# A fused encoder step on one NeuronCore: the first set of FF1 products in two parts, six of eight pairs of feature tiles first

## The chip, the cores and the metric

One Trainium2 chip, one of its cores. The metric is the device time of one execution in microseconds (us); every time below is of that kind. A change of 0.2% is 5.3 us.

## The reference, cut to what matters

One layer of a streaming encoder over 640 tokens (512 of a prompt, 8 x 16 of a decode step), model width 2048, feed-forward width 5632, all in float32:

```
o = concat(rmsnorm(oa, norm_grp_a), rmsnorm(ob, norm_grp_b))
x = x + o @ w_out
h = rmsnorm(x, norm_ffn)
x + (silu(h @ w_gate) * (h @ w_up)) @ w_down
```

`oa` and `ob` are the outputs of two groups of attention heads. What matters here is the seam between `o @ w_out` (the out-projection) and the first product with `w_gate`.

## The kernel before, in words

**Operands.** A float32 product is made of three matmuls (`mm3`, lines 175 to 179): each operand is split into a high part `hi` (ScalarE, line 168) and a rest `lo` (VectorE, line 169), and hi x hi (line 177), hi x lo (line 178) and lo x hi (line 179) are summed in one PSUM bank. Splitting weights gives two tiles of 128 x 1024, splitting activations two of 128 x 320.

**Out-projection.** The second half of the out-projection (lines 833 to 849) makes 16 feature tiles `m` in the order 0, 8, 1, 9, ..., 7, 15. Each takes 48 matmuls over eight operand tiles (`own_a`, 16 slots in SBUF), writes two banks of the PSUM pool `dn`, and is then read out by VectorE (line 841), added to the residual `x2[m]` (line 842), stored, and squared and summed (line 247 on ScalarE, line 248 on GpSimd). In time the last three tiles are m = 14, m = 7 and m = 15.

**Preparing pairs.** FF1 multiplies by Strassen's scheme in its seven-product form: the 16 feature tiles are taken as eight pairs (`kt`, `kt + 8`), each token row is cut in two halves, and every pair gives seven left operands (`prepare`, lines 798 to 831): two scalings by the gain on ScalarE (line 802), four additions on VectorE (lines 820, 821, 823, 825), and seven splits. A left operand fills one SBUF slot, so a pair needs seven. Pairs 0 to 4 are prepared inside the out-projection, as soon as both tiles of the pair are there. Pairs 5, 6 and 7 are prepared step by step between the first seven FF1 products (`prep`, line 911; pair 7 in place, in its own `x2` tiles and one more).

**The FF1 products.** `quartet` (lines 856 to 908) loads four weight blocks of 512 KB (`get`, line 876), forms combinations of them (lines 889 and 891 on VectorE, 893 and 900 on GpSimd) and yields seven products in the order p1, p6, p7, p2, p5, p4, p3. Each product splits its weights into two slots of a list `H` (four slots at first, six after the first set), then runs 8 x 3 = 24 matmuls, one triple for each pair, so the first set is 168 matmuls. p1 and p5 lie in one two-bank tile of `dn`, p6 and p3 in another, p7, p2 and p4 in single banks of the pool `at` (four banks). After each product its bank is read out (line 949 on ScalarE, line 910 on VectorE). The first set is `w_gate` of FF tile pair 0; behind it come the sums for the norm (line 221, matmuls of one column, and later line 233, which spreads the result), then the set `w_up` of the same pair, which begins with its own p1 and p6.

**Slots set the order of the loads.** SBUF slots come from first-in-first-out lists: `n.get` takes the oldest free slot, `n.put` appends one, in the order of the program text. `W` (128 x 1024) holds weight blocks and the copies that `prepare` works on; a load into a slot starts when the last reader of the slot's former tile is done. At the first set the list has eight slots; call them A and B (the raw buffers of the out-projection's weights) and a0 to a5. In program order the blocks b12, b22, b11 and the combination s6 take A, B, a4 and a5, pairs 5 and 6 take a0, a1 and a2, a3, and b21 takes A again once b12 is split. The set `w_up` then gets A and B for b12 and b22, a0 (pair 5's) for b11 and a2 (pair 6's) for b21.

**Queues.** All loads and stores are issued by SyncE's one queue, in order. The framework under the kernel orders each engine's instructions at build time: by program order as priority and by a modelled time of readiness. On the chip each engine's queue runs in that order.

Of the kernel before, what the change touches and what calls it, by code (L numbers as in the profile page):

```python
# [8 lines left out]
ALU = mybir.AluOpType  # L9
# [6 lines left out]
KT = 16  # L16
TOK = 640
HT = 320
# [251 lines left out]
def build(nc, tc, io, pools):  # L270
    n = Net(nc, tc, io, pools)
    dma = nc.sync.dma_start
# [522 lines left out]
    more = group_operands(oa_d, g_a, ssq_a, range(4, 8))  # L795
    own_a, acts_a = own_a + more[0], acts_a + more[1]

    def prepare(kts, in_place=()):

        work = []  # L800
        for kt in kts:
            scale = lambda t, m: nc.scalar.activation(t[:, :TOK], x2[m], AF.Identity, scale=g_ffn[:, m:m + 1])
            if kt in in_place:
                a, c, e = x2[kt], x2[kt + 8], n.get("S")
                s1, s2 = e[:, :HT], e[:, HT:]
                drop = ("S", a, c, e)
            else:
                a, c = n.get("W"), n.get("W")
                s1, s2 = a[:, TOK:TOK + HT], c[:, TOK:TOK + HT]
                drop = ("W", a, c)  # L810
            scale(a, kt)
            scale(c, kt + 8)
            if kt not in in_place:
                n.put("S", x2[kt], x2[kt + 8])
            work.append((a[:, :HT], a[:, HT:TOK], c[:, :HT], c[:, HT:TOK], s1, s2, hs[kt], drop))
        tt = nc.vector.tensor_tensor
        for which in (0, 1, 2, 4, 3, 5, 6):
            for a11, a21, a12, a22, s1, s2, out, _ in work:
                if which == 1:
                    tt(s1, a21, a22, ALU.add)  # L820
                    tt(s2, s1, a11, ALU.subtract)
                elif which == 2:
                    tt(a11, a21, a11, ALU.subtract)
                elif which == 6:
                    tt(a12, a12, s2, ALU.subtract)
                t = n.get("S")
                out[which] = t, pack(t, HT)
                n.split((a11, s2, a11, s1, a12, a22, a12)[which], *out[which][1])
            yield which
        for w in work:  # L830
            n.put(*w[-1])

    hs = [[None] * 7 for _ in range(8)]
    x2 = [None] * KT
    for i, m in enumerate(m for kt in range(8) for m in (kt, kt + 8)):
        ps = n.dense([(io["w_out_a"][m], 8)], acts_a)
        if i == 0:
            n.rstd(ssq_a, 1024, r_a)
        d, x2[m] = n.get("S"), n.get("S")
        dma(out=x2[m], in_=x2_d[m])  # L840
        nc.vector.tensor_tensor(halves(d), ps, halves(r_a), ALU.mult)
        nc.vector.tensor_tensor(x2[m], x2[m], d, ALU.add)
        n.put("S", d)
        n.add_square(ssq, x2[m], i == 0, "S")
        dma(out=x2_d[m], in_=x2[m])
        if m >= 8 and m - 8 < 5:
            for _ in prepare([m - 8]):
                pass
    n.put("S", r_a, ssq_a, *own_a)


    n.move("WH", "H", 4)
    n.move("WR", "W1", 2)
    n.lists["W"] = n.lists.pop("W1") + n.lists["W"]

    def quartet(k, load, lefts, before=None, after=None, part="all"):

# [1 line left out]
        def product(src, which, bank):  # L861
            own = n.get("H"), n.get("H")
            hl = [r(sh(x, k, P)) for x in own]
            n.split(sh(src, k, P), *hl)
            if before:
                before(which)
            for j in range(k):
                n.mm3(bank, (hl[0][:, j], hl[1][:, j]), lefts[j][which][1], j == 0, j == k - 1)
            n.put("H", *own)
            if after:  # L870
                after(which)
            return bank
# [8 lines left out]
        if part == "late":  # L881
# [2 lines left out]
                yield name, product(src, which, n.bank()[:, :HT])  # L884
                n.put("W", src)
            return
        x, y = n.banks(), n.banks()
        b12, b22, b11 = get(1), get(3), get(0)
        nc.vector.tensor_tensor(b12[:, w], b12[:, w], b22[:, w], sub)  # L889
        s6 = n.get("W")  # L890
        nc.vector.tensor_tensor(s6[:, w], b11[:, w], b12[:, w], sub)  # L891
        yield "p1", product(b11, 0, x[:, 0])
        nc.gpsimd.tensor_tensor(b11[:, w], b22[:, w], s6[:, w], sub)  # L893
        yield "p6", product(s6, 1, y[:, 0])
        yield "p7", product(b12, 2, n.bank()[:, :HT])
        n.put("W", b12)
        b21 = get(2)
        if part == "all":
            yield "p2", product(b21, 4, n.bank()[:, :HT])
        nc.gpsimd.tensor_tensor(b21[:, w], b21[:, w], s6[:, w], sub)  # L900
        n.put("W", s6)
        yield "p5", product(b11, 3, x[:, 1])
        n.put("W", b11)
        yield "p4", product(b21, 5, n.bank()[:, :HT])
        n.put("W", b21)
        if part == "all":
            yield "p3", product(b22, 6, y[:, 1])
        n.put("W", b22)

    add = lambda o, a, b: nc.vector.tensor_tensor(o, a, b, ALU.add)  # L910
    prep = prepare([5, 6, 7], [7])
    lefts = [[None] * 7 for _ in range(NPAIR)]

    def fetch(j, which, raw=None, engine=nc.gpsimd):
# [25 lines left out]
    for i in range(NPAIR):  # L940
        for src in ("w_gate", "w_up"):
# [2 lines left out]
            y = n.get("S"), n.get("S")  # L944
            c11, c21, c12, c22 = y[0][:, :HT], y[0][:, HT:], y[1][:, :HT], y[1][:, HT:]
            start, end = i == 0 and src == "w_gate", i == NPAIR - 1 and src == "w_up"
            for step, bank in quartet(8, load, hs, (lambda w: next(prep)) if start else None, free if end else None):
                if step == "p1":
                    nc.scalar.activation(c11, bank, AF.Identity)
                elif step == "p6":  # L950
# [241 lines left out]
```

## Time and profile before

| | us |
|---|---|
| median of 3 runs | 2664.4 (2662.84 to 2664.69) |
| the profiled execution | 2662.34 |
| its span in the trace | 2660.6 |

TensorE's mean granted clock in the profiled execution was 0.992 of full speed. In the rows, PE is TensorE's matmuls, DVE VectorE, ACT ScalarE, POOL GpSimd, SPq SyncE's queue of transfers. A row of a timeline has its start and its length in us; the bracket at its end gives the engine's idle time just before it and what ended it. S, W, dn and at in a row are the lists and pools named above (H slots are W tiles too).

### The profile page before, as it was taken

The numbers are of one execution on the slowest core, as the hardware profiler recorded it, in microseconds if no ns is written. First come the engines' busy times: TensorE is split into PE (matmuls) and PEld (weight loads), VectorE is DVE, ScalarE is ACT, GpSimd is POOL, SyncE is SP. The second block draws the span as 40 slices with busy tenths as digits, with TensorE's granted clock in tenths as the row PEclk, the third lists the DMA queues.
The fourth block names the chain that finished last, engine by engine and source line by source line (L and its number), as shares of the span: only waits on it lengthen the run. The fifth ranks groups of instructions, "written<-read, shape, count | busy, mean of one in ns | idle before, by whom it ended". The sixth has DMA issues, their size and how long they took to land.

```text
span 2660.6 us, 44831 instructions
## 1 busy us (share of the span) xinstructions
PE 2588.9 (97%) x17565; PEld 2532.0 (95%) x17565; DVE 1916.3 (72%) x2961; ACT 1086.3 (41%) x1767; POOL 765.2 (29%) x553
## 2 busy tenths in 40 slices
PE   8999999999999999999999999999999999999986
PEld 8999998999899989999999999999999999999986
DVE  5665566656866887667667666676678888888897
ACT  5443344434634543333333333333334444444443
POOL 0000000000211223433343343334335434344454
PEclk9999999999999999999999999999999999999998
DMA  5322232433655433333333333323335744444344
GB/s 173 104 75 79 89 99 93 130 117 132 218 181 186 154 114 105 114 105 107 113 105 107 126 104 106 122 97 113 114 100 173 223 134 129 133 133 126 109 114 141
DMA packets 154147, 332.23 MB, mean 125 GB/s; under 512 B 18064, under 2 KB 69264, under 8 KB 153936
## 3 DMA queue, kind: packets, MB, share of 16 engines
q1 hardware_dynamic: 153936, 329.38, 39.1%
q8 instruction: 138, 2.26, 0.4%
q14 instruction: 73, 0.60, 0.1%
HBM read 274.38 MB, written 54.20 MB: 123 GB/s over the span
## 4 chain that ended last, share of the span: by engine, by line
PE 72%; DVE 6%; DMA 3%; issue 2%; ACT 1%; DVEq 0%; POOL 0%; SPq 0%; ACTq 0%
PE dn L177 15%; PE dn L179 15%; PE dn L178 14%; PE at L177 9%; PE at L178 9%; PE at L179 9%; DVE W L169 2%; DMA S<-act_d 1%; PE at L289 1%; DVE S L910 1%; DMA W<-w_down 1%; DVE S L1081 1%; ACT W L168 0%; DVE S L923 0%; PE at L365 0%
## 5 line engine op out<-in xcount | busy, mean ns | idle before, releaser
L177 PE MATMUL dn<-S,W 128*128 128x320 f32 x3694 | 1161.5, 314 | 14.8 <-ACT S L922 5.7
L179 PE MATMUL dn<-S,W 128*128 128x320 f32 x3694 | 1148.3, 311 | 11.1 <-DVE W L169 10.9
L178 PE MATMUL dn<-S,W 128*128 128x320 f32 x3694 | 1146.8, 310 | 2.0 <-DVE S L169 1.1
L168 ACT ACTIVATE W<-W 128x1024 fp32r<-128x1024 f32 (+2 forms) x632 | 608.8, 964 | 1051.3 <-PE dn L178 532.1
L169 DVE TENSOR_TENSOR W<-W,W 128x1024 fp32r<-128x1024 f32 (+2 forms) x632 | 766.1, 1212 | 150.0 <-ACT W L168 145.8
L177 PEld LDWEIGHTS dn<-S,W 128*128 128x128 f32 x3694 | 697.4, 189 | 28.4 <-issue 8.5
L179 PEld LDWEIGHTS dn<-S,W 128*128 128x128 f32 x3694 | 697.1, 189 | 15.9 <-DVE W L169 14.7
L178 PEld LDWEIGHTS dn<-S,W 128*128 128x128 f32 x3694 | 697.3, 189 | 4.7 <-DVE S L169 1.3
L179 PE MATMUL at<-S,W 128*128 128x320 f32 x1594 | 493.6, 310 | 6.7 <-DVE W L169 6.5
L177 PE MATMUL at<-S,W 128*128 128x320 f32 x1594 | 493.0, 309 | 0.0
L178 PE MATMUL at<-S,W 128*128 128x320 f32 x1594 | 492.7, 309 | 0.0
L893 POOL TENSOR_TENSOR W<-W,W 128x1024 f32<-128x1024 f32 (+2 forms) x76 | 163.4, 2149 | 583.1 <-DVE W L169 481.4
L179 PEld LDWEIGHTS at<-S,W 128*128 128x128 f32 x1594 | 299.3, 188 | 8.9 <-DVE W L169 8.7
L177 PEld LDWEIGHTS at<-S,W 128*128 128x128 f32 x1594 | 299.6, 188 | 0.3 <-ACT W L168 0.3
L178 PEld LDWEIGHTS at<-S,W 128*128 128x128 f32 x1594 | 299.4, 188 | 0.0
L910 DVE TENSOR_TENSOR S<-S,dn 128x320 f32<-128x320 f32 x358 | 164.0, 481 | 97.8 <-PE dn L179 96.5
L889 DVE TENSOR_TENSOR W<-W,W 128x1024 f32<-128x1024 f32 (+2 forms) x76 | 134.1, 1764 | 97.1 <-DMA W<-w_up 51.1
L900 POOL TENSOR_TENSOR W<-W,W 128x1024 f32<-128x1024 f32 (+2 forms) x76 | 166.4, 2190 | 111.0 <-DVE W L169 105.9
L910 DVE TENSOR_TENSOR S<-S,at 128x320 f32<-128x320 f32 x262 | 123.2, 480 | 71.0 <-PE at L179 71.0
L248 POOL TENSOR_TENSOR S<-S,S 128x640 f32<-128x640 f32 x40 | 76.4, 1909 | 155.6 <-ACT S L247 152.4
L891 DVE TENSOR_TENSOR W<-W,W 128x1024 f32<-128x1024 f32 (+2 forms) x76 | 82.1, 1080 | 32.3 <-DMA W<-w_gate 25.2
L503 POOL MEMSET S<- 80x640 f32 x9 | 6.3, 695 | 329.2 <-DMA ob_d<-S 211.7
(147 smaller groups left out, 2255.1 us busy)
## 6 DMA issues: line engine op xcount, KB each, us to landing
W<-w_gate SPq DMA_DIRECT2D x88, 512.0 KB
W<-w_up SPq DMA_DIRECT2D x88, 512.0 KB
W<-w_in SPq DMA_DIRECT2D x66, 512.0 KB
W<-w_down SPq DMA_DIRECT2D x64, 384.0 KB
W<-w_down SPq DMA_DIRECT2D x68, 320.0 KB
act_d<-S SPq DMA_DIRECT2D x66, 320.0 KB
half<-act_d SPq DMA_DIRECT2D x81, 160.0 KB
S<-act_d SPq DMA_DIRECT2D x80, 160.0 KB
```

Of the source, the lines that this page charges most:

```text
L168: self.nc.scalar.activation(hi, src, AF.Identity)
L169: self.nc.vector.tensor_tensor(lo, src, f(hi), ALU.subtract)
L177: mm(out, a[0], b[0], start=first, stop=False)
L178: mm(out, a[0], b[1], start=False, stop=False)
L179: mm(out, a[1], b[0], start=False, stop=last)
L248: (eng or nc.gpsimd).tensor_tensor(ssq, ssq, sq, ALU.add)
L289: nc.tensor.transpose(out, src, n.ident)
L889: nc.vector.tensor_tensor(b12[:, w], b12[:, w], b22[:, w], sub)
L891: nc.vector.tensor_tensor(s6[:, w], b11[:, w], b12[:, w], sub)
L893: nc.gpsimd.tensor_tensor(b11[:, w], b22[:, w], s6[:, w], sub)
L900: nc.gpsimd.tensor_tensor(b21[:, w], b21[:, w], s6[:, w], sub)
L910: add = lambda o, a, b: nc.vector.tensor_tensor(o, a, b, ALU.add)
```

## The change

The first set runs as two sets. The first takes pairs 0 to 5 and leaves seven banks open (the two `dn` tiles and three of `at`, all taken beforehand); its weight blocks are 128 x 768. The second takes pairs 6 and 7, with blocks of 128 x 256, adds into the same banks, closes them, and only its products are read out. Pair 5 is prepared in the program text of the last out-projection tile, behind its fifth operand tile; the slots of `own_a` are given back there two by two, and the slot of `ssq_a` early. Pairs 6 and 7 are prepared between the products of the first part.

```diff
+    EARLY = 6
...
+    def last_early():
+
+        for k in range(8):
+            n.put("S", *own_a[2 * k:2 * k + 2])
+            if k == 4:
+                for _ in prepare([EARLY - 1]):
+                    pass
+            yield
+
...
+        if m == KT - 1:
+            n.rate = 1.0
+            n.add("heads", last_early())
         ps = n.dense([(io["w_out_a"][m], 8)], acts_a)
         if i == 0:
             n.rstd(ssq_a, 1024, r_a)
+            n.put("S", ssq_a)
...
-        if m >= 8 and m - 8 < 5:
+        if m >= 8 and m - 8 < EARLY - 1:
...
-    n.put("S", r_a, ssq_a, *own_a)
+    n.drain()
+    n.put("S", r_a)
...
-    def quartet(k, load, lefts, before=None, after=None, part="all"):
+    def quartet(k, load, lefts, before=None, after=None, part="all", banks=None, opened=False):
...
-                n.mm3(bank, (hl[0][:, j], hl[1][:, j]), lefts[j][which][1], j == 0, j == k - 1)
+                n.mm3(bank, (hl[0][:, j], hl[1][:, j]), lefts[j][which][1], j == 0 and not opened,
+                      j == k - 1 and (opened or not banks))
...
-    prep = prepare([5, 6, 7], [7])
+    prep = prepare([6, 7], [7])
...
-            for step, bank in quartet(8, load, hs, (lambda w: next(prep)) if start else None, free if end else None):
+            if start:
+                b = n.banks(), n.banks()
+                banks = {"p1": b[0][:, 0], "p6": b[1][:, 0], "p5": b[0][:, 1], "p3": b[1][:, 1]}
+                banks.update((name, n.bank()[:, :HT]) for name in ("p7", "p2", "p4"))
+                for _ in quartet(EARLY, lambda z: load(z)[:, :EARLY], hs, lambda w: next(prep), banks=banks):
+                    pass
+                steps = quartet(8 - EARLY, lambda z: load(z)[:, EARLY:], hs[EARLY:], banks=banks, opened=True)
+            else:
+                steps = quartet(8, load, hs, None, free if end else None)
+            for step, bank in steps:
```

## Rows read from the trace of the kernel before

**Rows 1.** The page's line of busy time, share of the span, instructions

```profile
PE 2588.9 (97%) x17565; PEld 2532.0 (95%) x17565; DVE 1916.3 (72%) x2961; ACT 1086.3 (41%) x1767; POOL 765.2 (29%) x553
```

**Rows 2.** Stretches: length, PE busy (matmuls), granted clock, DMA share, GB/s

```profile
955.50:958.60 3.10, 3.10 (x23) 1.00 0.05 21
958.60:967.70 9.10, 5.79 (x21) 0.63 0.44 152
967.70:988.20 20.50, 19.59 (x132) 1.00 0.32 104
...
993.20:998.00 4.80, 2.90 (x23) 1.00 0.34 109
```

**Rows 3.** Timeline of PE across the seam and into the set w_up

```profile
958.45 0.31 PE L179 MATMUL dn<-S,W 128*128 128x320 f32 x1
960.58 0.42 PE L177 MATMUL dn<-S,W 128*128 128x320 f32 x1 [1.82 <-ACT S L168]
962.05 0.63 PE L178 MATMUL dn<-S,W 128*128 128x320 f32 x1 [1.06 <-DVE S L169]
...
963.92 0.64 PE L179 MATMUL dn<-S,W 128*128 128x320 f32 x1 [0.44 <-DVE W L169]
...
988.13 1.39 PE L221 MATMUL at<-cst,S 128*128 128x1 f32 x12
...
989.75 0.31 PE L179 MATMUL dn<-S,W 128*128 128x320 f32 x1
...
992.83 0.31 PE L179 MATMUL dn<-S,W 128*128 128x320 f32 x1
...
995.33 0.42 PE L179 MATMUL dn<-S,W 128*128 128x320 f32 x1 [1.90 <-DVE W L169]
```

**Rows 4.** Timeline of DVE in the same stretch

```profile
949.08 1.22 DVE L889 TENSOR_TENSOR W<-W,W 128x1024 f32<-128x1024 f32 x1 [2.24 <-DMA W<-w_gate]
...
955.75 2.70 DVE L169 TENSOR_TENSOR S<-W,S 128x320 fp32r<-128x320 f32 x1
...
960.79 0.81 DVE L841 TENSOR_TENSOR S<-dn,S 128x640 f32<-128x640 f32 x1
...
981.94 1.22 DVE L169 TENSOR_TENSOR W<-W,W 128x1024 fp32r<-128x1024 f32 x1
...
990.84 3.24 DVE L169 TENSOR_TENSOR W<-W,W 128x1024 fp32r<-128x1024 f32 x1
```

**Rows 5.** Timeline of POOL beside the slow DVE row

```profile
955.44 2.66 POOL L893 TENSOR_TENSOR W<-W,W 128x1024 f32<-128x1024 f32 x1
```

**Rows 6.** The stretch in which DVE never rests: length, then each engine's busy time (instructions)

```profile
949.08:983.16 34.08, 29.86 (x180) 28.33 (x180) 33.36 (x45) 18.26 (x32) 11.09 (x4) 0.90 0.29 98
```

**Rows 7.** Groups by form: busy us and mean ns of one | idle before

```profile
L169 DVE TENSOR_TENSOR W<-W,W 128x1024 fp32r<-128x1024 f32 x13 | 15.8, 1217 | 0.0
L823 DVE TENSOR_TENSOR W<-W 128x320 f32<-128x320 f32 x6 | 2.9, 480 | 0.0
L168 ACT ACTIVATE W<-W 128x1024 fp32r<-128x1024 f32 x13 | 13.8, 1059 | 18.6 <-PE dn L178 14.8 <-issue 3.8
L900 POOL TENSOR_TENSOR W<-W,W 128x1024 f32<-128x1024 f32 x3 | 7.2, 2416 | 11.0 <-DVE W L169 11.0
L974 POOL TENSOR_TENSOR S<-S,S 128x640 f32<-128x640 f32 x2 | 3.1, 1588 | 2.7 <-ACT S L973 2.7
```

**Rows 8.** SyncE's queue: issues of weight blocks

```profile
960.89 0.33 SPq L876 DMA_DIRECT2D W<-w_up  x1
...
981.26 0.33 SPq L876 DMA_DIRECT2D W<-w_up  x1
983.18 0.33 SPq L876 DMA_DIRECT2D W<-w_up  x1
```

**Rows 9.** Chain of waits: start, length, what the chain went through

```profile
944.55 4.43 DMA W<-w_gate
...
983.18 4.75 DMA W<-w_up
```

More of the change, by code (lines that the diff above doesn't have):

```diff
@@ L838, in build @@
             n.rstd(ssq_a, 1024, r_a)
+            n.put("S", ssq_a)
         d, x2[m] = n.get("S"), n.get("S")
-        dma(out=x2[m], in_=x2_d[m])
+        x = x2[m]
+        dma(out=x, in_=x2_d[m])
         nc.vector.tensor_tensor(halves(d), ps, halves(r_a), ALU.mult)
-        nc.vector.tensor_tensor(x2[m], x2[m], d, ALU.add)
+        nc.vector.tensor_tensor(x, x, d, ALU.add)
         n.put("S", d)
-        n.add_square(ssq, x2[m], i == 0, "S")
-        dma(out=x2_d[m], in_=x2[m])
-        if m >= 8 and m - 8 < 5:
+        n.add_square(ssq, x, i == 0, "S")
+        dma(out=x2_d[m], in_=x)
+        if m >= 8 and m - 8 < EARLY - 1:
             for _ in prepare([m - 8]):
                 pass
-    n.put("S", r_a, ssq_a, *own_a)
+    n.drain()
+    n.put("S", r_a)
     n.move("WH", "H", 4)
@@ L886, in quartet @@
             return
-        x, y = n.banks(), n.banks()
+        if not banks:
+            x, y = n.banks(), n.banks()
+            banks_of = {"p1": x[:, 0], "p6": y[:, 0], "p5": x[:, 1], "p3": y[:, 1]}
+        else:
+            banks_of = banks
+        bank_of = lambda name: banks_of[name] if name in banks_of else n.bank()[:, :HT]
         b12, b22, b11 = get(1), get(3), get(0)
@@ L891, in quartet @@
         nc.vector.tensor_tensor(s6[:, w], b11[:, w], b12[:, w], sub)
-        yield "p1", product(b11, 0, x[:, 0])
+        yield "p1", product(b11, 0, bank_of("p1"))
         nc.gpsimd.tensor_tensor(b11[:, w], b22[:, w], s6[:, w], sub)
-        yield "p6", product(s6, 1, y[:, 0])
-        yield "p7", product(b12, 2, n.bank()[:, :HT])
+        yield "p6", product(s6, 1, bank_of("p6"))
+        yield "p7", product(b12, 2, bank_of("p7"))
         n.put("W", b12)
@@ L898, in quartet @@
         if part == "all":
-            yield "p2", product(b21, 4, n.bank()[:, :HT])
+            yield "p2", product(b21, 4, bank_of("p2"))
         nc.gpsimd.tensor_tensor(b21[:, w], b21[:, w], s6[:, w], sub)
         n.put("W", s6)
-        yield "p5", product(b11, 3, x[:, 1])
+        yield "p5", product(b11, 3, bank_of("p5"))
         n.put("W", b11)
-        yield "p4", product(b21, 5, n.bank()[:, :HT])
+        yield "p4", product(b21, 5, bank_of("p4"))
         n.put("W", b21)
         if part == "all":
-            yield "p3", product(b22, 6, y[:, 1])
+            yield "p3", product(b22, 6, bank_of("p3"))
         n.put("W", b22)
     add = lambda o, a, b: nc.vector.tensor_tensor(o, a, b, ALU.add)
-    prep = prepare([5, 6, 7], [7])
+    prep = prepare([6, 7], [7])
     lefts = [[None] * 7 for _ in range(NPAIR)]
@@ L946, in build @@
             start, end = i == 0 and src == "w_gate", i == NPAIR - 1 and src == "w_up"
-            for step, bank in quartet(8, load, hs, (lambda w: next(prep)) if start else None, free if end else None):
+            if start:
[5 more added lines that the diff above has]
+                steps = quartet(8 - EARLY, lambda z: load(z)[:, EARLY:], hs[EARLY:], banks=banks, opened=True)
+            else:
+                steps = quartet(8, load, hs, None, free if end else None)
+            for step, bank in steps:
                 if step == "p1":
```

## The prediction

> **What bounds the kernel now.** I read the page's busy line first: TensorE (PE) is busy for 97% of the span and VectorE (DVE) for 72% [rows 1]. So anything to be won lies where PE waits. The table of stretches then shows the seam between out-projection and FF1: full clock and no gap up to 958.6, then 9.1 us with only 21 matmuls at a mean granted clock of 0.63, so in part at 1.2 of 2.4 GHz, then full work again except for single gaps [rows 2]. The timeline of PE names the waits [rows 3]. At 958.45 the last matmul starts that has its operands. The next waits for a ScalarE (ACT) split of an activation until 960.58, the one after it for the matching DVE split until 962.05, and the one at 963.92 for the low part of p6's weights. Later p6 of the set w_up waits 1.90 us for its low part, until 995.33.
>
> How much is lost? The 22 starts from 989.75 to 992.83 lie 146.7 ns apart (21 steps in 3.08 us) [rows 3], so the first set, 168 matmuls, is 24.6 us of work. Of p1, 21 matmuls (pairs 0 to 6) ran before the first gap: 3.1 us, so the out-projection ended at 955.5. The first set's end is where the norm's sums start, 988.13 [rows 3]. 988.1 - 955.5 - 24.6 = 8.0 us lost in the set; with the 2.0 us of w_up's p6 it is 10.0 us. That is all that the seam can give back.
>
> What makes PE wait is DVE. From 949.08 to 983.16, where the last low part of the set is ready (981.94 + 1.22) [rows 4], it is busy for 33.4 of 34.1 us [rows 6]: the read-out of two out-projection tiles, the splits of pairs 5 to 7 and seven weight splits, in one queue. p1 needs one operand of all eight pairs, so it waits for pair 7. The read-out of m = 15, whose bank p6 wants, came only at 960.79 [rows 4], five us after its matmuls.
>
> **The change, part by part.**
>
> *p1 to p3 on six pairs.* The wait for pair 7 leaves p1. What the first 18 matmuls of each product need is pair 5, whose slots are the four free ones and the first three of `own_a`; those come free from about 949.5, when m = 15 has read its first operand tile. PE can go on from 955.5, and its own bound for the end of the set is 955.5 + 24.6 = 980.1, which is 8.0 us earlier than now.
>
> *DVE's work.* It does not shrink. Nine DVE operations on 1024 columns (seven splits, lines 889 and 891) become nine on 768 and nine on 256. 1217 ns for 1024 columns and 480 for 320 [rows 7] give 1.05 ns a column and 0.14 us for the instruction itself: 9 x 0.14 = +1.3 us. One split of pair 5 can move ahead of 949.08 into idle time: -0.5 us. So the last low part is ready at 983.2 + 1.3 - 0.5 = 984.0, and then only 6 matmuls are left, 0.9 us, where 24 were. By DVE's bound the set ends at 984.9, 3.2 us earlier than now. Between -8.0 and -3.2 I take -3.2, since DVE rested for 0.7 us in 34 [rows 6] and nothing is taken from it.
>
> *ACT, POOL, transfers.* Seven ACT splits in two parts cost some 1.4 us on an engine busy 18.3 of 34.1 [rows 6]: hidden, and if DVE were no bound, ACT would still not be one. Two POOL operations become four: 2416 ns for 1024 columns and 1588 for 640 [rows 7] give 2.2 ns a column and 0.2 us each, +0.4 us on POOL, 11.1 busy of 34.1. Four loads become eight: four more issues of 0.33 us [rows 8] on a queue that mostly waits. The second part's blocks go into slots that are free from about 960 to 970, well before their use at about 974. The early return of `ssq_a` and `n.drain` issue nothing. Pair 5's splits are now ahead of the read-out of m = 15 in program order; behind them on DVE stand lines 889 and 891 and p1's weights, some 0.95 us each by the line above, and m = 7's read-out, 2 x 0.81: 4.5 us of work in the 6.4 us from 949.1 to 955.5, so they are due in time only if pair 5 takes no more than 1.9.
>
> *DVE beside POOL.* A split of 320 columns took 2.70 us, not 0.48, while POOL's line 893 ran beside it, and both ended within 0.4 us of each other [rows 4, 5, 7]. Such losses are in the 33.4 us, and I leave them as they are. The Trainium skill (SBUF — State Buffer, Who interferes with whom) says that a DVE operation with two SBUF inputs and a GpSimd one exclude each other for a whole instruction. By it the two new POOL operations, 0.8 us each by the line above, could each hold up one DVE operation, an estimate of +1.5 us on the sum.
>
> *The opening of w_up.* This is where I see most of the gain go. Following the list of slots through the new text: pair 5 takes a4 and a5 in the last tile, part one takes A, B, a0, a1 and (for b21) a4, part two a5, A, a1, a0 and a4. The set w_up then gets a0 for b12, a1 for b22 and a4 for b11. All three are last read by part two: a0 as its s6, a1 as its b11, a4 as its b21. Before, b11 was issued at 960.89 [rows 8], and only b12 and b22 late, at 981.26 and 983.18. Now b11's load waits for the split of part two's p4. That comes before the last split by 0.4 us and about two read-outs of 0.48: 984.0 - 1.4 = 982.6. A load of 512 KB lands 4.43 to 4.75 us after its issue [rows 9]; three are under way at once, so 4.75: 987.4. Then ACT's split, 1.06 us [rows 7]: p1 starts at 988.5. DVE first makes s6 (1.2 us), then p1's low part (1.2): 989.8, from where p1 runs its other 22 matmuls until 993.0. p6's low part follows on DVE at 991.0, or 993.0 if POOL stretches it as it did at 990.84, where two splits took 3.24 us [rows 4]. So p6's low part is used at about 993.4, where it was 995.33: -1.9 us in place of -3.2. PE waits in between from 986.2 (set end and 1.25 us of sums) to 988.5 and again 1 us: about the waits of 958.6 to 962.05, after which the stretch shows 0.63 of full clock. Half clock over the 16 matmuls or so that had it there costs 16 x 0.12 = 1.9 us; the single 2 us wait before 995.33 came out of a stretch at 1.00 [rows 2]. Between 0 and 1.9 I take 0.5, nearer to none, since these waits are shorter. Landing is bounded below by 4.43 us and above by three loads one after the other, 3 x 4.43 from about 981: 994.
>
> The Trainium skill (DMA: Bandwidth & Descriptors, Anatomy of one DMA) prices a load at about 2.0 us plus its bytes at 436 GB/s, an estimate of 3.2 us for 512 KB. By it the sum would be 1.5 us lower; the rows show 4.4 to 4.8, and the sum goes by them.
>
> **Sum.** -1.9 + 0.5 = -1.4 us. The profiled execution took 2662.34 us, 1.7 us around its span; it lies 2.06 below the median of the runs, 2664.4. On the median: 2663.0.
>
> **The rivals.**
>
> *B, PE's bound holds.* DVE puts read-outs and pairs 6 and 7 into gaps, and the set ends near 981. For it: only pair 7 stood at the head of the first wait, and from 967.7 on PE lost less than 1 us [rows 2]. Against: DVE's 33.4 of 34.1. The late slots still hold: b11 issued at about 979, landed at 983.8, p6 at 990 in place of 995.3: -5.5 us, 2658.9. Chance 0.2.
>
> *C, slower.* The three loads at w_up's opening share the queue and land as late as 991 (two of them moved 1.05 MB in 6.7 us [rows 8, 9]; a third at that rate needs 10 us from 981). Then p1's low part is ready at 993.4, its 22 matmuls run at half clock, 5.9 us, and p6 starts at 999.3: +4 us, and with the added POOL holds +5.5: 2669.9. It decides from a landing after about 989. For it: all three slots are late by the list. Against: two loads together took hardly longer than one. The Trainium skill (TensorE: Matmul & The Clock Gate, HAM oscillation) describes waits for a transfer after which matmuls restart at half clock; 958.6 to 967.7 agrees. Chance 0.1.
>
> *D, the seam stays.* Pair 5's slots come free no earlier than now, DVE's queue keeps the read-out of m = 15 late, and p6 waits in place of p1, with the half clock after it: what is won later pays for it. 0 us, 2664.4. For it: DVE's queue is the same length. Against: p1 no longer waits for pair 7. Chance 0.2.
>
> **How the numbers follow.** The forecast has 0.5; its own range is 2660 to 2666. 0.2% of 2664.4 is 5.3 us, about what a measurement of this kernel can tell from no change. B lies at that line and counts as faster for most of its chance: 0.18. C counts as slower for most: 0.08. The rest, 0.74, is within. The range takes in the forecast, D, most of B and the near side of C: 2657.5 to 2668.
>
> **What would show it.** In the changed trace: p1 to p3 of part one without a gap and at full clock from 955.5; the last low part near 984 and line 221's sums near 985 (B: 981, D: 988); three `w_up` issues within 2 us shortly before, b11's the last; a wait of PE of 2 to 3.5 us ahead of w_up's p1 and none ahead of p6. If w_up's loads are issued before 978, or the set ends before 982, the sum is wrong on the fast side; if the granted clock is low for more than 5 us behind 986, on the slow side.

## The result, and the profile of the changed kernel

The change makes the kernel slower by about 5 us: 2669.6 us (median of 15 runs, 2666.81 to 2671.22) against 2664.4 (15 runs, 2661.82 to 2665.69). The ratio is 1.0019, with an interval of 1.0011 to 1.0027: wholly above 1, and about at the 0.2% that the prediction took as its line. The forecast was 2663.0, and the range ended at 2668.0.

The profiled execution took 2670.63 us with a span of 2668.9; that of before took 2662.34. Its busy line answers to [rows 1]:

```profile
PE 2595.9 (97%) x17565; PEld 2538.5 (95%) x17565; DVE 1914.0 (72%) x2970; ACT 1086.6 (41%) x1774; POOL 768.2 (29%) x555
```

PE has the same 17565 matmuls and is busy 7 us longer: part of the loss is matmuls that ran slowly. DVE is busy 2 us less, where the prediction had added 1.3.

To place the loss, I read the same event in both timelines. The read-out of m = 14 starts at 941.71 before and 942.50 after, 0.8 later; over the fourteen traces of this document it lies between 940.59 and 944.78, so these 0.8 us say nothing on the change. ScalarE's read-out of p1 in the fourth of the FF1 sets starts at 1046.86 before and 1053.93 after. So from the one to the other it is 105.15 us before and 111.43 after: **+6.3 us at the seam**. From there to 2065 the shift stays at 7.1; another 1.2 us comes in the last product. The 0.8 and the 1.2 make up the 8.3 us between the two profiled executions and are not traced to anything in the change.

The table of stretches (columns as in [rows 2], with all engines: length, then busy time of PE, weight loads, DVE, ACT and POOL, granted clock, DMA share, GB/s) shows two holes:

```profile
960.00:970.00 10.00, 6.35 (x25) 6.10 (x26) 7.95 (x16) 7.41 (x16) 3.12 (x1) 0.66 0.37 117
...
990.00:1000.00 10.00, 5.26 (x27) 4.60 (x27) 8.04 (x13) 6.57 (x9) 3.38 (x2) 0.84 0.34 130
```

The first hole is the old one, in the first set, with 25 matmuls in 10 us. The second, at the opening of w_up, with 27 matmuls, is nearly all new. The timeline of PE, to be held against [rows 3]:

```profile
958.87 0.31 PE L179 MATMUL dn<-S,W 128*128 128x320 f32 x1
961.95 0.41 PE L177 MATMUL dn<-S,W 128*128 128x320 f32 x1 [2.77 <-ACT W L168]
...
964.20 0.64 PE L179 MATMUL dn<-S,W 128*128 128x320 f32 x1 [1.70 <-DVE W L169]
964.63 0.47 PE L177 MATMUL dn<-S,W 128*128 128x320 f32 x1
...
969.43 0.37 PE L177 MATMUL at<-S,W 128*128 128x320 f32 x1
...
990.31 0.31 PE L179 MATMUL dn<-S,W 128*128 128x320 f32 x1
991.52 1.55 PE L233 MATMUL at<-cst,sm 128*128 128x128 f32 x12 [0.90 <-DVE sm L228]
994.55 0.41 PE L177 MATMUL at<-S,W 128*128 128x320 f32 x1 [1.47 <-ACT W L168]
997.47 0.63 PE L179 MATMUL at<-S,W 128*128 128x320 f32 x1 [2.37 <-DVE W L169]
997.90 0.47 PE L177 MATMUL at<-S,W 128*128 128x320 f32 x1
```

*First set.* The 18 matmuls of p1 run without a gap until 958.87, as forecast. Then p6 waits, first for its high part (ACT, line 168), then for its low part (DVE, line 169), and 18 steps of 0.267 us at half clock follow, to 969.43. From 958.87 to 964.63 there are 5.76 us for four steps of 0.147: 5.2 us lost; the half clock adds 18 x 0.12 = 2.2. The set begins at 958.87 - 17 x 0.147 = 956.4 and ends at 990.5, with the norm's sums (1.25) inside: 34.1 us, where before it was 955.5 to 989.4, 33.9. It gained nothing.

*Opening of w_up.* From 990.31 to 1003.50 PE runs 25 matmuls and the 12 small ones of line 233, which took 1.3 us in the trace of before: 25 x 0.147 + 1.3 = 5.0 us of work in 13.2, so 8.2 lost, 21 x 0.12 = 2.5 of it by half clock (997.90 to 1003.50). Before, the loss there was the one wait of 2 us ahead of 995.33 [rows 3]. The difference of 6.2 is the seam's +6.3. The waiting matmuls at 994.55 and 997.47 write a bank of `at`: the set opens with p7 and not, as before, with p1.

What held p6 stands in three timelines of the changed kernel. That of DVE answers to [rows 4]:

```profile
954.84 1.87 DVE L169 TENSOR_TENSOR S<-W,S 128x320 fp32r<-128x320 f32 x1
956.89 2.28 DVE L169 TENSOR_TENSOR S<-W,S 128x320 fp32r<-128x320 f32 x2 [0.19 <-ACT S L168]
...
960.92 0.82 DVE L857 TENSOR_TENSOR S<-dn,S 128x640 f32<-128x640 f32 x1
...
963.20 0.95 DVE L169 TENSOR_TENSOR W<-W,W 128x768 fp32r<-128x768 f32 x1
```

That of ACT in the same stretch:

```profile
956.39 0.83 ACT L168 ACTIVATE S<-W 128x320 fp32r<-128x320 f32 x2 [1.60 <-POOL S L248]
959.61 0.83 ACT L168 ACTIVATE S<-W 128x320 fp32r<-128x320 f32 x2 [2.39 <-DVE W L827]
...
961.07 0.83 ACT L168 ACTIVATE W<-W 128x768 fp32r<-128x768 f32 x1
```

And that of POOL:

```profile
954.57 1.79 POOL L248 TENSOR_TENSOR S<-S,S 128x640 f32<-128x640 f32 x1 [7.76 <-ACT S L247]
956.32 2.10 POOL L917 TENSOR_TENSOR W<-W,W 128x768 f32<-128x768 f32 x1
```

The read-out of m = 15 (line 857, line 841 before) starts at 960.92, where it was 960.79 in [rows 4]: it did not move. p6's low part (963.20) stands behind it. ACT makes p6's high part at 961.07, behind pair 5's splits, and those wait for POOL's sum of squares (line 248) and for DVE. Each queue runs in order: on DVE and on ACT p6 stands behind pair 5, and pair 5 on ACT behind POOL.

What held the opening, first in SyncE's queue:

```profile
986.36 1.34 SPq L895 DMA_DIRECT2D W<-w_up  x3
```

then on DVE:

```profile
991.79 1.23 DVE L913 TENSOR_TENSOR W<-W,W 128x1024 f32<-128x1024 f32 x1 [0.32 <-DMA W<-w_up]
993.58 1.56 DVE L1005 TENSOR_TENSOR S<-S,S 128x640 f32<-128x640 f32 x2 [0.57 <-ACT S L235]
995.06 1.22 DVE L915 TENSOR_TENSOR W<-W,W 128x1024 f32<-128x1024 f32 x1
996.19 1.22 DVE L169 TENSOR_TENSOR W<-W,W 128x1024 fp32r<-128x1024 f32 x1
998.15 4.26 DVE L169 TENSOR_TENSOR W<-W,W 128x1024 fp32r<-128x1024 f32 x2 [0.73 <-ACT W L168]
```

and on ACT:

```profile
993.11 0.44 ACT L235 ACTIVATE S<-at 128x320 f32<-128x320 f32 x1 [0.23 <-PE at L233]
993.44 1.05 ACT L168 ACTIVATE W<-W 128x1024 fp32r<-128x1024 f32 x1
994.51 1.28 ACT L1006 ACT_TABLE_LOAD   x1
995.80 1.36 ACT L1006 ACTIVATE S<-S 128x640 f32<-128x640 f32 x2
997.08 1.99 ACT L168 ACTIVATE W<-W 128x1024 fp32r<-128x1024 f32 x2
```

Three of w_up's four loads are issued at 986.36 or later; line 913, which makes p7's weights (b12 - b22), starts at 991.79 on their landing and ends at 993.02. By then gate's finish is due. ACT splits p7's high part at 993.44, behind the norm's read-out (line 235). DVE makes its low part only at 996.19, 1.7 us after the high part was ready (994.49): gate's multiplications (line 1005) and line 915 stand ahead of it. The table load and Silu stand ahead of the splits of p1 and p6 (997.08), but PE is busy with p7 by then, and no row of PE behind 997.47 shows a wait for them. In the trace of before the table load stands at 997.85, behind the splits of p1, p7 and p6 (984.66, 989.22 and 990.56).

### The profile page after: what moved, and what is told of

It is laid out like the page before. It is cut to its first block, busy times and chain, and to the rows that moved or that the text cites. A ratio compares the mean times of both kernels' runs of the same rounds, so it can differ in the third digit from the quotient of the medians.

```text
span 2668.9 us, 44863 instructions
## 1 busy us (share of the span) xinstructions
PE 2595.9 (97%) x17565; PEld 2538.5 (95%) x17565; DVE 1914.0 (72%) x2970; ACT 1086.6 (41%) x1774; POOL 768.2 (29%) x555
## 4 chain that ended last, share of the span: by engine, by line
PE 70%; DVE 6%; DMA 3%; issue 2%; ACT 2%; POOL 1%; SPq 0%; DVEq 0%; POOLq 0%; ACTq 0%
PE dn L177 14%; PE dn L179 14%; PE dn L178 14%; PE at L177 9%; PE at L178 8%; PE at L179 8%; DVE W L169 2%; PE at L289 1%; DVE S L934 1%; DMA W<-w_down 1%; DMA S<-act_d 1%; DVE S L1114 1%; DMA S<-cva 0%; DVE S L947 0%; DVE S L169 0%
## 5 line engine op out<-in xcount | busy, mean ns | idle before, releaser
L168 ACT ACTIVATE W<-W 128x1024 fp32r<-128x1024 f32 (+3 forms) x639 | 609.9, 955 | 1055.3 <-PE dn L178 534.3
L169 DVE TENSOR_TENSOR W<-W,W 128x1024 fp32r<-128x1024 f32 (+3 forms) x639 | 763.2, 1195 | 157.4 <-ACT W L168 152.9
```

The costliest lines, as they stand in the source:

```text
L168: self.nc.scalar.activation(hi, src, AF.Identity)
L169: self.nc.vector.tensor_tensor(lo, src, f(hi), ALU.subtract)
```

## The experiments

All were timed in rounds with the kernel before on the same chip. Two numbers are read from each profile: from the read-out of m = 14 to p1's read-out in the third set ("to the third") and in the fourth ("to the fourth"). Before: 80.46 and 105.15; changed: 86.75 and 111.43. Each comes from one profiled execution; against before, they differ from what the medians say by up to 1.6 us, so a difference of that size or less shows nothing.

**Slots of w_up's loads.** The changed kernel with the list of slots turned behind the first set, so that w_up's loads go where they are free early:

```diff
+                n.lists["W"] = [n.lists["W"][k] for k in (4, 5, 6, 7, 0, 1, 2, 3)]
                 n.move("W", "H", 2)
```

> The changed kernel, but the set w_up takes its first blocks from slots that are free early (those of pair 6 and of part one's b22). Theory: in the changed kernel's trace TensorE loses 2.9 us to p6 of part one and about 2.8 us to the half clock behind it, and then 7.9 us in the opening of w_up (1.1 + 1.5 + 2.5 of waits, 2.8 of half clock), because w_up's three loads were issued only at 986.4 and the two splits of p1 and p6 stand behind the gate's Silu. With early slots the loads are issued before 982, TensorE loses under 2 us in the opening and keeps its full clock there; the first set stays as it is. Time: 2669.6 - 6 = about 2663.5, ratio to before 0.999 to 1.001. Rival (the opening is held by the queues of VectorE and ScalarE, not by the slots): 2668 to 2670, ratio 1.001 to 1.003.

Measured: 2668.44 us, ratio 1.0019 [1.001, 1.0028]; 85.37 and 111.91. (The 112.7 in two later expectations is a misreading of this 111.91.) The loads went out at 964.7, 968.4 and 979.4, and the fourth at 987.5, where three had gone out from 986.4; the time stayed, as the rival has it. p6 of the first set waited as before, and the opening found other waits: the norm's small operations on DVE came late, and a new wait came in the second w_up set. Line 913 waits there for a load that landed at 1036.76, against 1034.79 in the changed kernel; in both, and before, three loads of that set stand behind stores in SyncE's queue, so it is likely but not shown that my order of slots makes it wait:

```profile
997.45 2.02 PE L233 MATMUL at<-cst,sm 128*128 128x128 f32 x12 [1.92 <-DVE sm L228]
...
1039.17 0.41 PE L179 MATMUL dn<-S,W 128*128 128x320 f32 x1 [1.59 <-DVE W L169]
```

So late loads alone were not the whole cause. The same edit to the kernel before (its own order of slots) was to show what early loads are worth there:

> The kernel before (one part, pair 5 between the products), with only the slots of the set w_up changed: its b12, b22 and b11 come from the slots of pairs 5 and 6. Theory: the 2.0 us that p6 of w_up waits there go, the 8.0 us of the first set stay: 2662.4, ratio 0.9985 to 0.9998. Rival (VectorE makes p6 late in any case): no change, 0.9995 to 1.0005.

Measured: 2664.89, ratio 1.0007 [0.9998, 1.0015]; 80.52 and 105.21. No gain shows, as the rival has it: in place of the 1.90 us wait of w_up's p6 there is one of 1.40 us for a low part, at 985.63.

**Pair 5 away from the sum of squares.** The last tile gives pair 5 slots that the sum of squares does not hold; alone, and together with the slots of w_up:

```diff
             if k == 4:
+                s = n.lists["S"]
+                n.lists["S"] = s[:2] + s[4:] + s[2:4]
                 for _ in prepare([EARLY - 1]):
```

> The changed kernel, but pair 5 takes two old free slots and then slots of own_a, and not the slots that m = 7's sum of squares has to leave first. Theory: p6 of part one waits because its weight split stands on ScalarE behind pair 5's split into the slot of m = 7's squares, which GpSimd gave up only at 956.4. Without that wait p6 waits under 1.5 us, the clock stays full, and the first set ends about 4 us earlier; the opening of w_up stays as slow. Time 2665 to 2667, ratio to before 1.000 to 1.001. Rival (VectorE has too much work before p6, whatever the slots): p6 still waits 3 us or more in all, 2668 to 2670.

> Both edits of slots at once, two-part first set kept. Theory: the two losses are separate and add up: 2669.6 - 6 - 4 = about 2659.5, ratio to before 0.9975 to 0.999, faster than both kernels. Rival (the gain of one is lost to the other, VectorE being the bound of the whole seam): 2662 to 2664.

Measured: 2669.22, ratio 1.0021 [1.0013, 1.003], 85.77 and 110.46; both together 2667.6, 1.0017 [1.0008, 1.0026], 83.51 and 109.98. The first came out as its rival has it; the two together lie 3.6 us above even the rival's range. Alone, the edit only moved the wait on POOL to pair 6, and p6 waited 2.76 and 1.04 us, first, by the profile, for the bank that the read-out of m = 15 (line 859 there) frees:

```profile
960.03 0.61 PE L177 MATMUL dn<-S,W 128*128 128x320 f32 x1 [2.76 <-DVE S L859]
```

**One part again.** The set in one part, with pair 5 still prepared in the last tile:

```diff
-                for _ in quartet(EARLY, lambda z: load(z)[:, :EARLY], hs, lambda w: next(prep), banks=banks):
-                    pass
-                steps = quartet(8 - EARLY, lambda z: load(z)[:, EARLY:], hs[EARLY:], banks=banks, opened=True)
+            steps = quartet(8, load, hs, (lambda w: next(prep)) if start else None, free if end else None)
```

> The changed kernel with the first set in one part again, pair 5 still prepared in the last out-projection tile. The seam is measured from the read-out of m = 14 to the p1 read-out of the fourth set: 105.1 us before, 111.4 us after the change, 112.7, 110.5 and 110.0 us in the first three experiments. Theory (the two parts cost the time, the early pair 5 alone costs nothing): the seam returns to 104 to 106 us and the time to 2663 to 2665. Rival (pair 5 ahead of the last read-out costs it): the seam stays at 108 us or more, 2667 to 2670.

Measured: 2663.78, ratio 1.0001 [0.9992, 1.001]; 79.19 and 103.88. The early pair costs nothing: what costs is the form in two parts.

**Two parts on five pairs**, with nothing in the last tile (`EARLY = 5`, `prepare([5, 6, 7], [7])`):

> Two parts, but the first with the five pairs that are ready anyway; pairs 5, 6 and 7 are prepared between the products of part one as in the kernel before, nothing is moved into the last out-projection tile. Theory (p6 of part one waits because pair 5 stands ahead of the read-out of m = 15 and of p6's weights on VectorE and ScalarE): p6 waits under 2 us, the seam is about 4 us shorter than after the change, 107 us, and the time 2665 to 2666. Rival (two parts alone cost it, by the read-outs and splits bunched in part two): p6 waits as before, 111 us, 2669.

Measured: 2673.0 (5 runs), ratio 1.0036 [1.0024, 1.0049]; 89.27 and 113.96, the slowest of all and slower than the rival's 2669; where the rest is lost was not followed up. p6 waits for the read-out of m = 15 (line 854 there) even with pair 5 no longer in the last tile; splits of 320 columns still stand ahead of it on DVE, three of them 4.05 us long together, from 953.20:

```profile
961.85 0.59 PE L177 MATMUL dn<-S,W 128*128 128x320 f32 x1 [2.74 <-DVE S L854]
```

**Another bank for p6.** p6 takes a bank that is free early and p4 that of m = 15; two slots of the last tile are held back until its end:

```diff
             if k == 4:
+                s = n.lists["S"]
+                late, n.lists["S"] = s[2:4], s[:2] + s[4:]
...
+            if k == 7:
+                n.lists["S"] += late
...
-                banks = {"p1": b[0][:, 0], "p6": b[1][:, 0], "p5": b[0][:, 1], "p3": b[1][:, 1]}
-                banks.update((name, n.bank()[:, :HT]) for name in ("p7", "p2", "p4"))
+                banks = {"p1": b[0][:, 0], "p4": b[1][:, 0], "p5": b[0][:, 1], "p3": b[1][:, 1]}
+                banks.update((name, n.bank()[:, :HT]) for name in ("p6", "p7", "p2"))
```

> The changed kernel with p6 in a single bank that the out-projection does not use (p4 takes p6's old one), and with the slots of m = 7's sum of squares and difference given out last, so that no split of pairs 5 or 6 waits for GpSimd's sum. Theory: two things hold p6 of part one, its bank (read out of m = 15 on VectorE) and its weights behind splits that wait for GpSimd; without both, p6 waits under 1.5 us and the clock stays full: the seam falls by 5 us or more to 106, the time to 2664. Rival (the work queued on VectorE holds p6's low part in any case): p6 still waits 3 us, the seam stays within 2 us of 111.

Measured: 2668.59, ratio 1.0017 [1.0008, 1.0026]; 85.87 and 110.56. The high part of p6 now runs at once, and its low part waits instead:

```profile
963.70 0.41 PE L179 MATMUL at<-S,W 128*128 128x320 f32 x1 [3.11 <-DVE W L169]
```

That is the rival: taking one gate away shows the next, and DVE's queue is behind the bank and behind the low part alike.

**Less work on DVE at the opening.** The slots of the first experiment, and the first set's read-outs off DVE (p6, p7 and p5 read out by ScalarE; p2, p4 and p3 left out of the sums). Then the same without the slots, the missing corner of four:

```diff
+                elif start:
+                    out = {"p6": c12, "p7": c21, "p5": c22}.get(step)
+                    if out is not None:
+                        nc.scalar.activation(out, bank, AF.Identity)
                 elif step == "p6":
                     add(c12, c11, bank)
```

> The first experiment (early slots for w_up), with the eight VectorE read-outs of the first set left out: p6, p7 and p5 are read by ScalarE alone, p2, p4 and p3 and the second read-out of p5 not at all, so the gate of FF tile pair 0 is not what the reference has. It takes 3.9 us from VectorE in the opening of w_up. Theory (with the loads early, the opening is bound by VectorE's bunched work of part two): TensorE's waits behind the first set fall from about 7 us to under 4, the seam from 112.7 to about 109.5. Rival (the order of the queues, not the amount of work, makes the waits): the seam changes by less than 1.5 us.

> The changed kernel, with the slots of w_up's loads as the change leaves them, but with VectorE's eight read-outs of the first set left out (p6, p7 and p5 are read out by ScalarE, p2, p4 and p3 not at all: that part of gate's products is left out of the sums). This is the missing corner of four: late loads with little VectorE work. Theory (the opening of w_up is held by either of two things, late loads or a crowd of work on VectorE, and only both cures together open it): the loads are still issued with the last splits of part two, ScalarE still puts gate's table load and Silu ahead of p1's split, PE waits there for more than 3 us and runs some 20 matmuls at half clock after it; from the read-out of m = 14 to p1's read-out of the fourth set 109 to 111 us (111.4 in the changed kernel, 107.7 with both cures), whole time some 2667.5 to 2669. Rival 1 (VectorE's work alone is the cause): 105 to 107.5 us, 2665 or less. In both, p6 of the first set still waits, since its read-outs lie behind that wait.

Measured: with early loads 2665.09, ratio 1.0003 [0.9994, 1.0012], 78.93 and 107.70; with late loads 2670.35, ratio 1.0022 [1.0013, 1.0031], 88.08 and 112.76. To the third set, where my order of slots does no harm yet, the four corners are:

| | DVE's work kept | DVE's read-outs left out |
|---|---|---|
| late loads | 86.75 | 88.08 |
| early loads | 85.37 | 78.93 |

Neither cure does anything much by itself; both together give back 7.8 us, more than the whole loss. (The kernel before does the read-outs that are left out here, so the last corner is no faster version of it.) With late loads and little DVE work the time is even 1.4 us above the theory's range. Three loads are issued from 984.71, and the timeline of PE at the opening looks as in the changed kernel:

```profile
994.47 0.64 PE L177 MATMUL at<-S,W 128*128 128x320 f32 x1 [1.47 <-ACT W L168]
...
997.39 0.64 PE L179 MATMUL at<-S,W 128*128 128x320 f32 x1 [2.02 <-DVE W L169]
```

But here DVE and ACT show that it is not the landing that ends these waits:

```profile
990.20 1.22 DVE L913 TENSOR_TENSOR W<-W,W 128x1024 f32<-128x1024 f32 x1
993.50 1.56 DVE L1009 TENSOR_TENSOR S<-S,S 128x640 f32<-128x640 f32 x2 [2.08 <-ACT S L235]
```

```profile
993.37 1.05 ACT L168 ACTIVATE W<-W 128x1024 fp32r<-128x1024 f32 x1
```

Line 913 starts at 990.20 without a wait for a load. ACT takes up its result 1.95 us after it is ready, behind the norm's read-out (line 235), and DVE makes the low part at 996.12, behind gate's multiplications (line 1009) and line 915. In the corner with both cures three of w_up's low splits stand ahead of gate's multiplications:

```profile
992.98 3.65 DVE L169 TENSOR_TENSOR W<-W,W 128x1024 fp32r<-128x1024 f32 x3 [0.81 <-ACT W L168]
996.55 3.77 DVE L1010 TENSOR_TENSOR S<-S,S 128x640 f32<-128x640 f32 x2
```

The edit of the slots thus came with two changes, an earlier landing and another order of the queues, which the framework makes at build time from modelled times. No run changes only one of them, so which of the two opens the set is not shown.

The rise of the last corner to the fourth set (107.70 - 78.93 = 28.77, where the others take 24.7 to 26.5) is the wait at the second w_up as in the first experiment: it ran into a wait of 2.54 us for DVE's line 169 at 1036.24, with half clock behind it.

**Less work on DVE at p6.** The low splits of pairs 4 and 5 left out, with pair 3's low part in their place; and then all reliefs together:

```diff
-                n.split((a11, s2, a11, s1, a12, a22, a12)[which], *out[which][1])
+                if early:
+                    hi = out[which][1][0]
+                    nc.scalar.activation(hi, (a11, s2, a11, s1, a12, a22, a12)[which], AF.Identity)
+                    out[which] = t, (hi, hs[3][which][1][1])
+                else:
+                    n.split((a11, s2, a11, s1, a12, a22, a12)[which], *out[which][1])
```

> The changed kernel, with VectorE's low splits of pairs 4 and 5 left out (14 operations of 320 columns; their matmuls use pair 3's low part, so this part of the products is left out of the result; the number of matmuls is the same). It takes some 7 us of work out of VectorE's queue around the last tile of out-projection, ahead of and just behind the read-out of m = 15, and takes nothing from ScalarE. Theory (the queue of VectorE, in order, is what p6 waits for: the read-out of m = 15 for its bank, then its own low part): p6 of the first set starts within 0.5 us of p1's last matmul, no half clock between 960 and 970, the set ends 5 to 8 us earlier than in the changed kernel (some 983 to 985 against 990.4 on its scale), and the opening of w_up, whose loads move with the set's end, still loses 6 to 8 us; from the read-out of m = 14 to p1's read-out of the fourth set 103.5 to 106.5 us (111.4 in the changed kernel), whole time 2661 to 2664.5. Rival 1 (ScalarE or the slots hold p6): p6 waits for ScalarE as long as before, 110 to 112 us, 2668 to 2670. Rival 2 (what is won in the set is paid at the opening, since the loads stay where they are): the set ends earlier but the sum stays at 109 to 112 us.

> The changed kernel with all reliefs together: w_up's loads in slots that are free early, the eight read-outs of the first set off VectorE, and no low splits of pairs 4 and 5 on VectorE (the parts of the computation named at these two runs are left out). Theory (VectorE's queue at the two places and the late loads are the whole of the loss): neither p6 of the first set nor the opening of w_up loses more than 1.5 us; from the read-out of m = 14 to p1's read-out of the third set some 8 to 10 us less than in the kernel before; to the fourth, where the order of slots costs 4 us at the second w_up, 97.5 to 101.5 us (105.1 before, 111.4 changed); whole time 2655 to 2660. Rival (a further gate of ScalarE or GpSimd follows): over 103 us, and over 2661.

Measured without the low parts: 2666.46, ratio 1.0012 [1.0003, 1.0021]; 82.56 and 107.25. The seam is 4.2 us shorter than in the changed kernel, 0.75 short of what the theory gave at least, and between it and the rivals. The first set takes 31.2 us (954.9 to 986.1) in place of 34.1: 2.9 won there, not 5 to 8. The timeline of PE:

```profile
959.19 0.39 PE L177 MATMUL dn<-S,W 128*128 128x320 f32 x1 [1.47 <-ACT S L168]
...
959.96 0.41 PE L179 MATMUL dn<-S,W 128*128 128x320 f32 x1 [0.24 <-DVE W L169]
```

The profile puts the first wait down to a split of ACT that ended at 959.07. But that split (S<-S, at 958.62) is one of pair 7, which p6 of part one doesn't read. Within 0.02 us of it, at 959.05, ended the read-out of m = 15 on DVE, which frees p6's bank:

```profile
955.90 0.49 DVE L828 TENSOR_TENSOR W<-W 128x320 f32<-128x320 f32 x1 [1.98 <-ACT S L833]
...
958.23 0.82 DVE L863 TENSOR_TENSOR S<-dn,S 128x640 f32<-128x640 f32 x1
```

It stands behind an addition of pair 5 that waited 1.98 us for ACT. The row of ACT that it waited for:

```profile
955.39 0.47 ACT L833 ACTIVATE S<-W 128x320 fp32r<-128x320 f32 x1 [2.04 <-POOL S L248]
```

and what POOL did before it:

```profile
951.20 2.37 POOL L923 TENSOR_TENSOR W<-W,W 128x768 f32<-128x768 f32 x1 [5.85 <-DVE W L169]
953.54 1.82 POOL L248 TENSOR_TENSOR S<-S,S 128x640 f32<-128x640 f32 x1
```

The wait for the low part shrank from 1.70 to 0.24 us: DVE's queue it was. But the read-out still comes late, now at the end of a chain: POOL's p5 weights (line 923), then its sum of squares, then pair 5's split on ACT, then pair 5's additions on DVE. The theory had DVE's work as the only gate; ACT behind POOL, which stalls DVE's queue, is the second.

All reliefs together: 2660.98, ratio 0.9989 [0.9981, 0.9998]; 75.56 and 103.90. That is 11.2 us less than the changed kernel to the third set, and 4.9 less than before, about half of the 8 to 10 expected; to the fourth it is the rival's "over 103". The opening of w_up is free of waits. What is left is the further gate that the rival named, the chain through POOL and ACT ahead of p6 (the read-out, line 863, ends at 959.56), with half clock behind it, and a wait at the second w_up. PE:

```profile
959.71 0.38 PE L177 MATMUL dn<-S,W 128*128 128x320 f32 x1 [1.51 <-ACT S L168]
...
1028.92 0.46 PE L179 MATMUL dn<-S,W 128*128 128x320 f32 x1 [1.85 <-DVE W L169]
```

and DVE ahead of the second wait, held by a load:

```profile
1026.50 1.23 DVE L919 TENSOR_TENSOR W<-W,W 128x1024 f32<-128x1024 f32 x1 [5.05 <-DMA W<-w_up]
```

**The same relief without leaving work out.** One part again, and the low splits of pairs 4 and 5 on GpSimd:

```diff
-                n.split((a11, s2, a11, s1, a12, a22, a12)[which], *out[which][1])
+                src, (hi, lo) = (a11, s2, a11, s1, a12, a22, a12)[which], out[which][1]
+                nc.scalar.activation(hi, src, AF.Identity)
+                (nc.gpsimd if early else nc.vector).tensor_tensor(lo, src, f(hi), ALU.subtract)
```

> Nothing is left out here: the changed kernel with the first set in one part again (pair 5 still prepared in the last tile), and with the low splits of pairs 4 and 5 (14 operations of 320 columns) made by GpSimd in place of VectorE. It asks whether VectorE's queue at the seam can be relieved without leaving work out, in the form that cost nothing. By the profile GpSimd is busy for some 12 of 42 us from 942 to 984 there and 14 operations of about 0.8 us fit beside that. Theory (VectorE's queue is the bound of the seam in either form, and 6.7 us taken off it come back in part): the waits of p1 shrink, the set ends 2 to 4 us earlier; from the read-out of m = 14 to p1's read-out of the fourth set 100 to 102.5 us (105.1 before, 103.9 with one part), whole time 2660 to 2662.5. Rival (VectorE's operations are stretched beside GpSimd's, as the read-out of m = 15 and the splits of 320 columns were, and GpSimd's own queue then holds pair 5's low part): 103.5 to 107 us, 2663 to 2667, and splits of 320 columns on VectorE of 1.5 us or more beside the added GpSimd rows.

Measured: 2665.29, ratio 1.0005 [0.9996, 1.0014]; 80.91 and 105.60, within the rival's range. DVE now waits 3 us for GpSimd, since pair 5's combinations are made in place and may not overwrite what GpSimd has yet to read, and PE waits longer in one piece than in any other kernel here:

```profile
966.17 0.64 PE L177 MATMUL dn<-S,W 128*128 128x320 f32 x1 [5.74 <-ACT S L832]
```

```profile
963.09 0.49 DVE L828 TENSOR_TENSOR W<-W 128x320 f32<-128x320 f32 x1 [3.06 <-POOL S L833]
```

No version without something left out beats the kernel before.

## Why the prediction was wrong

**The steps that held.** p1 of part one runs without a gap. Early pair 5 costs nothing, as the run in one part shows. The three w_up loads are issued within 2 us of each other, late, and behind part two's splits. The two added GpSimd operations took 0.74 us each, and no one waited for them longer than 0.55 us.

**The step that failed first: "by DVE's bound the set ends at 984.9".** I took DVE's sum of work over the stretch as its bound, since it rested for only 0.7 us in 34 [rows 6], and let the work be done in any order. The same length of stretch after the change:

```profile
949.88:983.96 34.08, 29.47 (x181) 28.68 (x180) 27.36 (x43) 16.37 (x33) 9.75 (x5) 0.90 0.27 87
```

DVE is busy for 27.4 of 34.1 us (32.1 of 39.4 up to the set's last low part, at 989.27, not 984.0), and the set ends no earlier. It did less than the sum and ended later: the sum is not what held the set. What counts is where in its in-order queue the next operand of PE stands. The prediction's sum has no wait of p6 in this set. Pair 7 left p1, and p6 took its place, at 5.2 us and 2.2 more of half clock: the read-out of m = 15 at 960.92 (960.79 before), then p6's low part at 963.20. The text held the warning: it gave pair 5 no more than 1.9 us ahead of the read-out "in time only if", and then did not price the other case. Beside POOL's lines 248 and 917, one split took 1.87 us and two took 2.28, against 0.48 for an operation of 320 columns in [rows 7], and ACT waited 1.60 and 2.39 us among them. That is rival D's mechanism, to the wait ("p6 waits in place of p1"), with half clock after it. Five pairs, other slots and another bank left a wait of p6 in place; taking work out of DVE's queue shortened it, as far as ACT behind POOL let it.

The Trainium skill (SBUF — State Buffer, Who interferes with whom) has a DVE operation with two SBUF inputs and a GpSimd one that reads SBUF shut each other out for a whole instruction, whichever comes first. The slow splits agree. The prediction applied it to the two new GpSimd operations alone, +1.5 us beside its sum; the collisions that cost were with GpSimd's old work (lines 248 and 917), beside which pair 5's splits, which p1 and p6 need, now run.

**The term that was mis-sized: the opening of w_up.** The prediction had a gain of 1.9 us, with 0.5 us back for half clock. Measured: 6.2 us lost against before.
- b11's load was set at 982.6, some 983.5 on the scale of the changed trace, whose set begins 0.9 later. The three went out from 986.36. Line 913 started on a landing at 991.79, some 5.4 us after the first issue; the prediction's 4.75 was near, its start was not. The price of 3.2 us that the prediction quotes is given by the Trainium skill (DMA: Bandwidth & Descriptors, Anatomy of one DMA) for the GpSimd path. These loads go by SyncE's queue, and the sum rightly left it out.
- The sum has p1 first, behind line 915 alone. In the trace p7 comes first, its high part behind the norm's read-out on ACT and its low part behind gate's multiplications and line 915 on DVE (996.19). No term had these: the queues at that place were not walked through.
- The row at 990.84 in [rows 4] was read as two splits in 3.24 us. It is one (x1), of p7's weights, since p6's high part was ready only at 991.62; p6's low part stood behind it, at 994.10.
- Half clock ran for 21 steps, 2.5 us, not 0.5.

It is rival C's place and condition ("a landing after about 989"), and the sign that the prediction gave for the slow side, a low clock for more than 5 us behind 986. That C's price fits too, 2669.9 against 2669.6 measured, is luck: its 5.5 us have p1 first and 1.5 us of holds by the added POOL work, and the trace shows neither. C held that the loads alone decide. The four corners say that it takes both cures: with early loads, DVE's crowd of splits, read-outs and the norm's small operations keeps PE waiting about as long.

**The chances.** C and D were taken as ways apart; the kernel did both, D in the first set and C at its end. The late slots, which the prediction had read correctly off the list, tie C to every case in which the first set doesn't end early: given D, C was a likely sequel and deserved more than 0.1 on its own. That last is argued from the list, not shown by a run.

**What stays open.** The 1.2 us in the last product and the 0.8 us ahead of the seam. Whether the landing of w_up's loads or the order of the queues that comes with their slots opens the set. Whether pair 5's combinations in slots of their own, not in place, would let GpSimd help: it wasn't tried.

## What to carry to other kernels

When a wait is taken from the head of an in-order engine's queue, walk that queue, and those of the engines that feed it, to the next operand that PE wants, and price that one; the sum of the queue's work did not say it here. Where two things are late together (a load and the engine that must treat it), removing one can show no gain, so cost them as a pair and test all four corners, and look whether an edit that moves a load also reorders the queues. A split of a set in two parts also moves the release of its buffers to the end: read off the list of slots which later loads then start together, and what the other engines are due to do at that moment.

## What was unexpected of the hardware

The same waits of PE did not always cost the clock. With the low parts of pairs 4 and 5 left out, p6 waited 1.47 us and then 0.24, and with all reliefs 1.51 and 0.25. The same 8 us of the two traces, first without the low parts and then with all reliefs:

```profile
958.00:966.00 8.00, 6.18 (x38) 5.58 (x38) 7.88 (x12) 5.70 (x11) 2.10 (x1) 1.00 0.30 99
```

```profile
958.00:966.00 8.00, 6.24 (x31) 5.82 (x30) 7.84 (x12) 5.75 (x11) 2.07 (x1) 0.79 0.25 83
```

The first kept 2.4 GHz; the second ran 13 steps of 0.267 us, at 1.2 GHz, and lost 1.6 us by it. Nor did the longer wait always cost it: with another bank for p6, PE waited 3.11 us, and the starts behind it lie 0.147 us apart. The Trainium skill (TensorE: Matmul & The Clock Gate, HAM oscillation) describes waits for a transfer after which matmuls restart at half clock; behind these waits, for other engines, one kernel of the three did so. Why just that one is open, so a prediction should hold both ends for such a wait.
